# Hybrid encoder block on one core: the second group's queries and keys projected chunk by chunk, each chunk followed by its two head pairs

## The chip, the core and the metric

The kernel runs on one core of one Trainium2 chip. The metric is the device time of one execution in microseconds (us). The kernel before took 1394.3 us (median of three runs, 1393.5 to 1394.34).

## The reference, cut to what matters

The block takes `x` of 256 tokens by 2048 channels. One input projection gives the operands of a recurrent branch (HGRN2), the queries, keys and values of an attention branch, and two gates. The two branches are projected back, weighted by the gates, summed and projected once more; a squared-ReLU MLP follows. The change touches the attention branch only:

```python
s = jnp.einsum('bhnqd,bhnkd->bhnqk', qc, kb).astype(jnp.float32) * (Dh ** -0.5) + bias[:, None]
s = jnp.where(valid[:, None, :], s, -jnp.inf)
p = jax.nn.softmax(s, axis=-1).astype(v.dtype)
o = jnp.einsum('bhnqk,bhnkd->bhnqd', p, vb)
```

There are 16 heads of 64 channels. Head h has a bias of its own, gathered from a table by relative distance.

## The kernel before, in words

**Arithmetic.** Every large product is made in split precision. A weight piece of 128 x 1024 numbers comes from DRAM into a `raw` tile, ScalarE rounds it to a high part (`wh`, line 91), and VectorE subtracts to get the low part (`wl`, line 92). `wh` and `wl` have four buffers each, `raw` has six. TensorE then multiplies high by high, high by low and low by high.

**Stages around the change.** After the recurrent branch come the attention's projections. A query or key *chunk* is 256 channels, that is four heads or two *head pairs*: `qk_chunk` streams 16 K-tiles of weights through TensorE (lines 177 and 182), 64 matmuls in all, and then evicts the sum into a tile `aq..T` or `ak..T` by one ScalarE copy (line 189) and two VectorE operations (190, 304). The two *groups* of the code are channels 0 to 511 (heads 0 to 7) and 512 to 1023 (heads 8 to 15). In the trace of the kernel before, `aq10T` is the first query chunk of the second group, `ak11T` its second key chunk. The loop before is: for each group, both query chunks, both key chunks, (in the first group) the value projection `av`, then the group's four head pairs. After the second group come the gate projections, of which `ga0` is the first (products on lines 135 to 137, named `acc_ga0c`).

**One head pair.** `attn_pair` writes the scores of two heads into the PSUM tile `s` (line 588, eight matmuls; the tile has one buffer). For each head, `attn_head` then loads the bias by a DMA that GpSimd issues (594) into one of three buffers, masks a corner (memset, 595), adds the bias to the two parts of the scores (597, 598), takes two maxima (600, 601), exponentiates with a running sum on ScalarE (603, 604), takes reciprocals (606) and scales (607, 608), all but 603 and 604 on VectorE. TensorE transposes the result in three pieces into `tpp` (611) and ScalarE copies that to `pt` (613). `attn_values` multiplies by the values into `pa` (624, eight matmuls), one pair later in the loop, and the result is split into `act_yb` (91, 92).

**What sets the order.** Each engine works through its own list of instructions in order. A scheduler writes these lists when the kernel is built; it moves independent work together, so a head pair's small operations stand among the large products of the code that follows it. Weight loads are issued by SyncE (`raw_..`), the bias loads by GpSimd. GpSimd also issues the accumulating transfers of a gate unit (line 789: `raw_ga0B` += `raw_ga0C`, and `rawd_ga0D` += `raw_ga0A`), each of 512 KB. A gate unit further copies one accumulator from PSUM on the way (`u_ga`, line 752), and the next product into the same pair of accumulators follows behind that copy.

In the trace and below the heads of the second group are called head 8 to head 15, and its pairs are pair 4 (heads 8 and 9) to pair 7 (heads 14 and 15).

Of the kernel before, what the change touches and what calls it, by code (L numbers as in the profile page):

```python
# [17 lines left out]
T = 256  # L18
# [4 lines left out]
NC = 512  # L23
# [9 lines left out]
C_HQ, C_HF, C_AQ, C_AK, C_GA, C_GB = 0, HG, 2 * HG, 3 * HG, 4 * HG, 4 * HG + D  # L33
# [17 lines left out]
def tile_hybrid_block(  # L51
# [38 lines left out]
    def split(hi, lo, src, copy=None):  # L90
        casts[:] = [(copy or nc.scalar.copy)(hi, src)]  # L91
        return nc.vector.tensor_tensor(lo, src, hi.bitcast(F32), op=ALU.subtract)  # L92
# [7 lines left out]
    def new_act(what):  # L100

        return apool.tile([P, 4, 2, T], F32R, name=f"act_{what}", tag="act")
# [60 lines left out]
    def gemm_t(rhs, w, n0, nkt, what):  # L163

        acc = new_acc(what)
        for a in weights(w, n0, nkt, T, what):
            tick(1)
            mm_t(acc, rhs, nkt, *a)
        return acc
# [45 lines left out]
    for kt, n in zip(starts, steps):  # L215
# [3 lines left out]
        with tc.high_priority(offset=2000):  # L219
            for j in range(n):  # L220
                g, hi = wmix[:, kt + j:kt + j + 1], xT[c][:, a + j, 0, :]
# [10 lines left out]
    def rows(factors, what):  # L232

        wide = hp.tile([P, NM, P], F32, name=f"wide_{what}", tag="wide", bufs=1)
        nc.vector.tensor_copy(wide, bc(factors, 2, P))
        tp = ps_tp.tile([P, NM, P], F32, name=f"tp_{what}", tag="tp")
        for m in range(NM):
            nc.tensor.transpose(tp[:, m, :], wide[:, m, :], ident)
        r = const.tile([P, T], F32, name=f"rows_{what}")
        nc.vector.tensor_copy(r, tp.rearrange("p m t -> p (m t)"))  # L240
        return r
# [50 lines left out]
    rstd_t = rows(rstd, "rstd")  # L292
    rstd8_t = const.tile([P, T], F32, name="rstd8_t")
# [7 lines left out]
    def z_t(col, what, dst, factor, acc=None):  # L301

        add_parts(dst, acc or gemm_t(xT, w_in_t, col, KD, what))
        nc.vector.tensor_tensor(dst, dst, bc(factor, 1, 2), op=ALU.mult)
        return dst
# [256 lines left out]
    acc_q = [gemm_t(xT, w_in_t, C_AQ + i * T, KD, f"aq0{i}") for i in range(2)]  # L562
# [12 lines left out]
    yb = []  # L575
    TOK = 11

    def qk_chunk(col, what, factor, acc=None):
        return z_t(col, what, bp.tile([P, 2, T], F32, name=f"{what}T", tag="qk", bufs=6), factor, acc)

    def attn_pair(g, pr, qT, kT):

        sc = ps_sc.tile([P, 2, NC], F32, name=f"s{g}{pr}", tag="sc")
        with tc.high_priority(offset=2000):
            for d, q, k in ((slice(0, P), slice(0, P), slice(0, P)), (slice(P, 3 * P), slice(P, T), slice(0, T))):
                for j in range(2):
                    r = slice(64 * j, 64 * j + 64)
                    nc.tensor.matmul(sc[:, j, d], qT[r, q], kT[r, k], start=True, stop=True)
        return [attn_head(g * 8 + 2 * pr + j, sc[:, j, 0:3 * P]) for j in range(2)]
# [26 lines left out]
    def attn_values(g, pr, pts, vs):  # L616

        hi, lo = yb[g][:, :, 0, :], yb[g][:, :, 1, :]
        po = ps_tp.tile([P, T], F32, name=f"pa{g}{pr}", tag="tp")
        with tc.high_priority(offset=2000):  # L620
            for i, src, dst in ((0, slice(0, 2), slice(0, T)), (1, slice(2, 3), slice(P, T))):
                for j, pt in ((1, pts[1]), (0, pts[0])):
                    r = slice(64 * j, 64 * j + 64)
                    nc.tensor.matmul(po[r, dst], vs[i][:, P * pr + 64 * j:P * pr + 64 * j + 64], pt[:, src, :].rearrange("p a t -> p (a t)"),
                                     start=i == 0, stop=i == 1, skip_group_check=True)
        split(hi[:, pr, :], lo[:, pr, :], po)
# [300 lines left out]
    av = [[None] * NM for _ in range(2)]  # L927
# [5 lines left out]
    def alone(u, then=None):  # L933
        run(u, then)
        flush()
        pairs.clear()

    for g in range(2):
        qT = [qk_chunk(C_AQ + g * NC + i * T, f"aq{g}{i}", rstd8_t, None if g else acc_q[i]) for i in range(2)]
        kT = [qk_chunk(C_AK + g * NC + i * T, f"ak{g}{i}", rstd_t) for i in range(2)]  # L940
        if not g:
            alone(Unit(lambda: xT, lambda: Sx, w_in_n, C_AV, "av", values))
        yb.append(new_act(f"yb{g}"))
        pts = None
        for pr in range(5):
            last = pts
            if pr < 4:
                pts = attn_pair(g, pr, qT[pr // 2][:, pr % 2, :], kT[pr // 2][:, pr % 2, :])
            if last:
                attn_values(g, pr - 1, last, av[g])  # L950

    ga, gb = [], []
    units = []
# [124 lines left out]
    for qd in range(NQ):  # L1078
        last = qd == NQ - 1
# [121 lines left out]
```

## Time and profile before

| | us |
|---|---|
| median of three runs | 1394.3 |
| the profiled execution | 1393.71 |
| its span (first to last instruction) | 1392.0 |
| TensorE clock granted in it | 0.998 |
| chunks of the second group, first matmul of `aq10` to last of `ak11` | 307 to 361 |
| gate unit `ga0`, from its first matmul to that of `ga2` | 361 to 415 |

Busy time and idle time are in microseconds, start times count from the span's start. TensorE's matmuls overlap, so a row's duration is longer than the distance to the next row: a wait on TensorE is read from the distance between two starts. Where the trace names a releaser in square brackets, the engine was idle for the time given there.

### The profile page before, as it was taken

What the parts mean: (1) busy time and instruction counts of PE and PEld (TensorE: products, weight loads), DVE (VectorE), ACT (ScalarE), POOL (GpSimd) and SP (SyncE); (2) the same over time, 40 slices, a digit from 0 to 9 for tenths busy, and PEclk for the clock granted to TensorE, in tenths of its full rate; (3) what the DMA queues carried; (4) which work ended last, traced back from release to release, by engine and by line L of the source; (5) the groups of instructions that cost most, each with busy time, mean ns of one, the idle gap of its engine ahead of it and who ended that gap; (6) DMA issues with size and microseconds to landing.
All of it is one profiled execution on the core that took longest, in us unless ns stands there. A gap on an engine that the chain in (4) does not pass through costs nothing.

```text
span 1392.0 us, 18634 instructions
## 1 busy us (share of the span) xinstructions
PE 1377.6 (99%) x6550; PEld 1142.7 (82%) x6550; DVE 1138.1 (82%) x1429; ACT 925.9 (67%) x1193; POOL 144.8 (10%) x231
## 2 busy tenths in 40 slices
PE   9999999999999999999999999999999999999997
PEld 7889888878778888888888888888888888888886
DVE  7897997975978785687998977879877897878885
ACT  6774765664766664346777776678666876668864
POOL 2000001100100000001211001100011001110200
PEclk9999999999999999999999999999999999999999
DMA  9654445784758896558989789997899888999892
GB/s 332 231 174 157 155 165 180 220 282 161 185 183 270 263 268 229 193 169 269 277 233 314 243 258 291 268 268 237 249 295 293 251 241 246 275 294 269 255 285 100
DMA packets 124078, 331.62 MB, mean 238 GB/s; under 512 B 11072, under 2 KB 11840, under 8 KB 123600
## 3 DMA queue, kind: packets, MB, share of 16 engines
q1 hardware_dynamic: 103696, 265.59, 54.1%
q0 software_dynamic: 19568, 64.04, 23.4%
q8 instruction: 51, 0.84, 0.2%
q10 hardware_dynamic: 720, 0.81, 0.2%
q14 instruction: 43, 0.35, 0.1%
HBM read 271.67 MB, written 10.49 MB: 203 GB/s over the span
## 4 chain that ended last, share of the span: by engine, by line
PE 93%; DVE 2%; issue 2%; DMA 1%; ACT 1%; POOL 0%; SPq 0%; POOLq 0%; ACTq 0%; DVEq 0%
PE acc_hf L177 2%; PE acc_ak L177 2%; PE acc_aq L177 2%; PE acc_hq L177 2%; PE ps L414 1%; PE tp_u L108 1%; PE acc_hg L136 1%; PE acc_bb L136 1%; PE acc_hg L135 1%; PE acc_ba L136 1%; PE acc_bb L137 1%; PE acc_ba L137 1%; PE acc_hg L137 1%; PE acc_bb L135 1%; PE acc_ba L135 1%
## 5 line engine op out<-in xcount | busy, mean ns | idle before, releaser
L177 PE MATMUL acc_aq<-act_x,wh_aq 128*128 128x512 f32 x128 | 41.8, 406 | 0.0
L177 PE MATMUL acc_hf<-act_x,wh_hf 128*128 128x512 f32 x128 | 41.0, 402 | 0.2 <-DVE wh_hf L91 0.2
L177 PE MATMUL acc_hq<-act_x,wh_hq 128*128 128x512 f32 x128 | 40.7, 399 | 0.0
L177 PE MATMUL acc_ak<-act_x,wh_ak 128*128 128x512 f32 x128 | 40.5, 397 | 0.1
L91 ACT CAST wh_bb<-raw_bb 128x1024 fp32r<-128x1024 f32 x16 | 16.9, 1054 | 23.3 <-PE acc_ba L137 17.7
L92 DVE TENSOR_TENSOR wl_bb<-raw_bb,wh_bb 128x1024 fp32r<-128x1024 f32 x16 | 19.6, 1223 | 14.8 <-ACT wh_bb L91 14.8
L91 ACT CAST wh_ba<-raw_ba 128x1024 fp32r<-128x1024 f32 x16 | 16.8, 1053 | 21.0 <-PE acc_bb L137 13.8
L92 DVE TENSOR_TENSOR wl_ba<-raw_ba,wh_ba 128x1024 fp32r<-128x1024 f32 x16 | 19.6, 1224 | 12.7 <-ACT wh_ba L91 12.7
L91 ACT CAST wh_aq<-raw_aq 128x1024 fp32r<-128x1024 f32 x16 | 16.8, 1051 | 19.4 <-PE acc_hg L137 8.8
L182 PEld LDWEIGHTS acc_hq<-act_x,wl_hq 128*128 128x128 f32 x128 | 23.4, 188 | 6.5 <-DVE wl_hq L92 1.3
L182 PEld LDWEIGHTS acc_hf<-act_x,wl_hf 128*128 128x128 f32 x128 | 23.4, 188 | 6.1 <-DVE wl_hf L92 0.9
L182 PEld LDWEIGHTS acc_ak<-act_x,wl_ak 128*128 128x128 f32 x128 | 23.5, 188 | 5.5 <-issue 0.3
L182 PEld LDWEIGHTS acc_aq<-act_x,wl_aq 128*128 128x128 f32 x128 | 23.6, 189 | 5.0
L92 DVE TENSOR_TENSOR wl_aq<-raw_aq,wh_aq 128x1024 fp32r<-128x1024 f32 x16 | 19.6, 1223 | 9.2 <-ACT wh_aq L91 9.2
L92 DVE TENSOR_TENSOR wl_hf<-raw_hf,wh_hf 128x1024 fp32r<-128x1024 f32 (+2 forms) x21 | 20.4, 969 | 6.9 <-ACT wh_hf L91 6.8
L91 ACT CAST wh_hf<-raw_hf 128x1024 fp32r<-128x1024 f32 (+1 forms) x19 | 16.9, 890 | 13.5 <-PE acc_hg L137 6.0
L92 DVE TENSOR_TENSOR wl_ak<-raw_ak,wh_ak 128x1024 fp32r<-128x1024 f32 x16 | 19.6, 1222 | 7.7 <-ACT wh_ak L91 7.7
L135 PE MATMUL acc_hi<-wh_hi,act_x 128*128 128x512 f32 x64 | 25.8, 403 | 0.0
L92 DVE TENSOR_TENSOR act_u<-tp_u,act_u 128x512 fp32r<-128x512 f32 x32 | 22.0, 686 | 4.7 <-ACT act_u L91 4.2
L98 POOL TENSOR_TENSOR ro<-ms,mhalf 128x2 f32<-128x2 f32 x8 | 5.9, 738 | 190.2 <-DVE ms L97 190.2
L135 PE MATMUL acc_hg<-wh_hg,act_x 128*128 128x512 f32 x64 | 25.7, 401 | 0.0
L182 PE MATMUL acc_hq<-act_x,wl_hq 128*128 128x256 f32 x128 | 24.7, 279 | 0.9 <-DVE wl_hq L92 0.9
(1928 smaller groups left out, 5267.4 us busy)
## 6 DMA issues: line engine op xcount, KB each, us to landing
raw_hi<-in_w_in_n_dram SPq DMA_DIRECT2D x16, 512.0 KB, 4.0
raw_hg<-in_w_in_n_dram SPq DMA_DIRECT2D x16, 512.0 KB, 3.6
raw_aq<-in_w_in_t_dram SPq DMA_DIRECT2D x16, 512.0 KB, 4.1
raw_ak<-in_w_in_t_dram SPq DMA_DIRECT2D x16, 512.0 KB, 3.6
raw_ba<-in_w_branch_a_dram SPq DMA_DIRECT2D x16, 512.0 KB, 4.6
raw_bb<-in_w_branch_b_dram SPq DMA_DIRECT2D x16, 512.0 KB, 4.6
raw_hf<-in_w_in_t_dram SPq DMA_DIRECT2D x12, 512.0 KB, 3.6
raw_hq<-in_w_in_t_dram SPq DMA_DIRECT2D x12, 512.0 KB, 3.7
```

What stands on the lines that cost most here:

```text
L91: casts[:] = [(copy or nc.scalar.copy)(hi, src)]
L92: return nc.vector.tensor_tensor(lo, src, hi.bitcast(F32), op=ALU.subtract)
L98: nc.gpsimd.tensor_tensor(dst, ms, mhalf[:, :width], op=ALU.pow)
L108: nc.tensor.transpose(tp[:, j, :], src[:, j * P:(j + 1) * P], ident)
L135: nc.tensor.matmul(acc, hi, wh, start=first, stop=False, skip_group_check=True)
L136: nc.tensor.matmul(acc, hi, wl, start=False, stop=False, skip_group_check=True)
L137: nc.tensor.matmul(acc, lo, wh, start=False, stop=last, skip_group_check=True)
L177: nc.tensor.matmul(acc[:, cb, :], wh[:, cb * P:(cb + 1) * P], r.rearrange("p u t -> p (u t)"), start=kt == 0, stop=last)
L182: nc.tensor.matmul(acc[:, cb, 0:T], wl[:, cb * P:(cb + 1) * P], r[:, 0, :], start=False, stop=False)
L414: nc.tensor.matmul(ps[:, m, :], klf[:, a * P:(a + 1) * P], qrf[:, a * 192:(a + 1) * 192], start=True, stop=True)
```

## The change

The loop over groups becomes a loop over chunks. The first group's four chunks are projected first as before, with the value projection behind them. The first group's head pairs follow in the same order. In the second group the third query chunk and the third key chunk (channels 512 to 767) are projected and followed by pairs 4 and 5; then the fourth chunks (channels 768 to 1023), followed by pairs 6 and 7. The product with the values still comes one pair later, now also across the border between groups. The tiles are named `aq0T` to `aq3T` and `ak0T` to `ak3T`; before's `aq10T` is after's `aq2T`, `aq11T` is `aq3T`, `ak10T` is `ak2T` and `ak11T` is `ak3T`. No instruction is added or removed.

```diff
-    for g in range(2):
-        qT = [qk_chunk(C_AQ + g * NC + i * T, f"aq{g}{i}", rstd8_t, None if g else acc_q[i]) for i in range(2)]
-        kT = [qk_chunk(C_AK + g * NC + i * T, f"ak{g}{i}", rstd_t) for i in range(2)]
-        if not g:
+    qT = [qk_chunk(C_AQ + i * T, f"aq{i}", rstd8_t, acc_q[i]) for i in range(2)]
+    kT = [qk_chunk(C_AK + i * T, f"ak{i}", rstd_t) for i in range(2)]
+    pts = None
+    for i in range(4):
+        if i > 1:
+            qT.append(qk_chunk(C_AQ + i * T, f"aq{i}", rstd8_t))
+            kT.append(qk_chunk(C_AK + i * T, f"ak{i}", rstd_t))
+        if not i:
             alone(Unit(lambda: xT, lambda: Sx, w_in_n, C_AV, "av", values))
-        yb.append(new_act(f"yb{g}"))
-        pts = None
-        for pr in range(5):
-            last = pts
-            if pr < 4:
-                pts = attn_pair(g, pr, qT[pr // 2][:, pr % 2, :], kT[pr // 2][:, pr % 2, :])
+        if not i % 2:
+            yb.append(new_act(f"yb{i // 2}"))
+        for pr in (2 * i, 2 * i + 1):
+            last, pts = pts, attn_pair(pr // 4, pr % 4, qT[i][:, pr % 2, :], kT[i][:, pr % 2, :])
             if last:
-                attn_values(g, pr - 1, last, av[g])
+                attn_values((pr - 1) // 4, (pr - 1) % 4, last, av[(pr - 1) // 4])
+    attn_values(1, 3, pts, av[1])
```

How the instruction lists move is seen at three places.

**TensorE, the chunk in which pair 5's scores are made.** Before, this is the fourth key chunk (`acc_ak` with `ak10T` ready); `s_3655` are pair 5's scores, and nothing of the softmax follows them in the chunk:

```order
L177 MATMUL acc_ak_3513<-act_x_109,wh_ak_8_3559 128x512
L588 MATMUL s_3655<-ak10T,aq10T 128x128 x2
L588 MATMUL s_3655<-ak10T,aq10T 128x256 x2
L177 MATMUL acc_ak_3513<-act_x_109,wh_ak_8_3559 128x512
L182 MATMUL acc_ak_3513<-act_x_109,wl_ak_8_3560 128x256 x2
L177 MATMUL acc_ak_3513<-act_x_109,wh_ak_8_3559 128x512 x2
```

After, it is the fourth query chunk (`acc_aq`), and `s_3469` are pair 5's scores; `tpp_3434` and `tpp_3456` are the transposes of heads 8 and 9, `pa_3462` the first group's last product with the values:

```order
L177 MATMUL acc_aq_3526<-act_x_109,wh_aq_8_3572 128x512
L588 MATMUL s_3469<-ak2T,aq2T 128x128 x2
L588 MATMUL s_3469<-ak2T,aq2T 128x256 x2
L611 MATMUL tpp_3434<-ident,sb_3421 128x128 x3
L177 MATMUL acc_aq_3526<-act_x_109,wh_aq_8_3572 128x512
L182 MATMUL acc_aq_3526<-act_x_109,wl_aq_8_3573 128x256 x2
L177 MATMUL acc_aq_3526<-act_x_109,wh_aq_8_3572 128x512 x2
L611 MATMUL tpp_3456<-ident,sb_3443 128x128
L624 MATMUL pa_3462<-pt_3217,av_2968 64x256
```

The transposes of heads 8 to 11 all move from the gate unit `ga0` into the fourth query chunk; the fourth key chunk behind it is left without any attention work.

**TensorE, the end of the product `ga0p21B`, where `u_ga` is copied.** `ga0r_8` is the next product; before, its first matmul stands directly behind `ga0p21B`:

```order
L136 MATMUL acc_ga0c_3852<-wl_ga0p21B_4022,S_x 128x512
L137 MATMUL acc_ga0c_3852<-wh_ga0p21B_4021,S_x 128x512
L135 MATMUL acc_ga0c_3852<-wh_ga0r_8_4041,act_x_109 128x512
L611 MATMUL tpp_3788<-ident,sb_3775 128x128
L136 MATMUL acc_ga0c_3852<-wl_ga0r_8_4042,act_x_109 128x512
```

After, pair 7's product with the values (`pa_3823`) stands between the two:

```order
L136 MATMUL acc_ga0c_3852<-wl_ga0p21B_4022,S_x 128x512
L137 MATMUL acc_ga0c_3852<-wh_ga0p21B_4021,S_x 128x512
L624 MATMUL pa_3823<-pt_3814,av_3004 64x256
L624 MATMUL pa_3823<-pt_3792,av_3004 64x256
L624 MATMUL pa_3823<-pt_3814,av_3006 64x128
L624 MATMUL pa_3823<-pt_3792,av_3006 64x128
L135 MATMUL acc_ga0c_3852<-wh_ga0r_8_4041,act_x_109 128x512
```

So independent work has come between the product whose sum is copied and the product that goes on with it.

**GpSimd, around the accumulating transfers of `ga0`.** `bias_3738`, `bias_3772` and `bias_3794` are the biases of heads 13, 14 and 15:

```order
 L789 DMA raw_ga0B_3834<-raw_ga0C_3838 128x1024
-L595 MEMSET bias_3716 64x64
 L789 DMA raw_ga0B_3836<-raw_ga0C_3840 128x1024
 L789 DMA rawd_ga0D_3842<-raw_ga0A_3830 128x1024
+L594 DMA bias_3794<-in_rel_bias_dram 128x256
 L789 DMA rawd_ga0D_3844<-raw_ga0A_3832 128x1024
-L594 DMA bias_3738<-in_rel_bias_dram 128x256
-L595 MEMSET bias_3738 64x64
-L594 DMA bias_3772<-in_rel_bias_dram 128x256
-L595 MEMSET bias_3772 64x64
-L594 DMA bias_3794<-in_rel_bias_dram 128x256
 L595 MEMSET bias_3794 64x64
```

The loads for heads 13 and 14 have moved ahead of all four accumulating transfers, and the load for head 15 now stands behind one transfer of `rawd_ga0D` and ahead of the other.

## The prediction, made before the changed kernel ran

> **What bounds the kernel now.** First the page: busy shares, the granted clock, and the chain that ended last.
>
> ```profile
> PE 1377.6 (99%) x6550; PEld 1142.7 (82%) x6550; DVE 1138.1 (82%) x1429; ACT 925.9 (67%) x1193; POOL 144.8 (10%) x231
> ...
> PEclk9999999999999999999999999999999999999999
> ...
> PE 93%; DVE 2%; issue 2%; DMA 1%; ACT 1%; POOL 0%; SPq 0%; POOLq 0%; ACTq 0%; DVEq 0%
> ```
>
> TensorE carries the chain almost from end to end at an undisturbed clock. As the change leaves the number of instructions on every engine as it was, the only thing it can move is the time TensorE waits. So the second view is the windows of 10 us around the attention (columns: stretch, its length, then busy us and count for PE, PEld, DVE, ACT, POOL; clock, DMA share, GB/s).
>
> ```profile
> 310.00:320.00 10.00, 10.00 (x67) 7.18 (x63) 8.50 (x27) 7.36 (x23) 1.51 (x5) 1.00 0.47 144
> ...
> 340.00:350.00 10.00, 10.00 (x60) 8.76 (x58) 5.03 (x7) 4.13 (x5) 0.00 (x0) 1.00 0.60 206
> 350.00:360.00 10.00, 10.00 (x63) 7.91 (x63) 9.23 (x18) 4.65 (x10) 3.12 (x6) 1.00 0.49 119
> ...
> 370.00:380.00 10.00, 9.79 (x49) 7.39 (x48) 9.79 (x21) 8.09 (x15) 1.80 (x3) 1.00 1.00 234
> 380.00:390.00 10.00, 8.77 (x51) 6.23 (x53) 8.18 (x23) 7.21 (x20) 1.43 (x4) 1.00 0.90 306
> ```
>
> In the second group's plain chunks (340 to 350) VectorE is half idle. In `ga0` (from 361) it is nearly full, because the softmax of heads 10 to 15 lies there beside the gate weights' splits, and TensorE falls under 10. In 310 to 320 a chunk carries two pairs of the first group, and TensorE is still at 10.00. The third view, TensorE's rows in order of time, gives the waits their size (start, duration).
>
> ```profile
> 361.67 0.40 PE L136 MATMUL acc_ga0c<-wl_ga0p11A,act_x 128*128 128x512 f32 x1
> 362.15 0.33 PE L611 MATMUL tpp<-ident,sb 128*128 128x128 f32 x1
> ...
> 379.39 0.40 PE L136 MATMUL acc_ga0c<-wl_ga0p21A,S_x 128*128 128x512 f32 x1
> 380.02 0.30 PE L611 MATMUL tpp<-ident,sb 128*128 128x128 f32 x1 [0.23 <-DVE sb L607]
> ...
> 383.90 0.48 PE L135 MATMUL acc_ga0c<-wh_ga0r,act_x 128*128 128x512 f32 x1
> 384.31 0.93 PE L588 MATMUL s<-ak11T,aq11T 64*128 64x128 f32 x8
> ...
> 387.56 0.39 PE L137 MATMUL acc_ga0c<-wh_ga0p21B,S_x 128*128 128x512 f32 x1
> 389.16 0.33 PE L611 MATMUL tpp<-ident,sb 128*128 128x128 f32 x1 [1.21 <-DVE sb L607]
> 389.42 0.87 PE L624 MATMUL pa<-pt,av 128*64 128x256 f32 x8
> 390.22 0.44 PE L611 MATMUL tpp<-ident,sb 128*128 128x128 f32 x2
> ...
> 391.42 0.39 PE L136 MATMUL acc_ga0c<-wl_ga0p21B,S_x 128*128 128x512 f32 x1
> 391.65 0.40 PE L137 MATMUL acc_ga0c<-wh_ga0p21B,S_x 128*128 128x512 f32 x1
> 392.72 0.49 PE L135 MATMUL acc_ga0c<-wh_ga0r,act_x 128*128 128x512 f32 x1 [0.67 <-ACT u_ga L752]
> 393.22 0.30 PE L611 MATMUL tpp<-ident,sb 128*128 128x128 f32 x1
> ```
>
> Undisturbed, one matmul of 512 columns starts 0.23 us after the last (391.42 to 391.65). What exceeds that in front of a row is lost: 1.37 (387.56 to 389.16), 0.84 (391.65 to 392.72), 0.40 (379.39 to 380.02), 0.27 (392.72 to 393.22), 0.25 (361.67 to 362.15) and 0.18 (383.90 to 384.31), **3.31 us** together. Part of it is the ordinary price of a turn to another kind of matmul:
>
> ```profile
> 349.94 0.39 PE L177 MATMUL acc_ak<-act_x,wh_ak 128*128 128x512 f32 x1
> 350.26 0.93 PE L588 MATMUL s<-ak10T,aq10T 64*128 64x128 f32 x8
> ...
> 354.80 0.93 PE L588 MATMUL s<-ak10T,aq10T 64*128 64x128 f32 x8
> ```
>
> A turn to scores that wait for nothing costs 0.32 - 0.23 = 0.09. Five of the six places are turns (not 391.65), so 0.45 stays in any order, and **2.86 us is all that the change can win**.
>
> **Why TensorE waits there.** The largest wait is for head 13's scaling (607), which VectorE reaches only after head 14's bias has come. GpSimd's rows:
>
> ```profile
> 371.69 0.60 POOL L594 DMA_DIRECT2D bias<-in_rel_bias_dram  x1
> 380.04 0.19 POOL L595 MEMSET bias<- 64x64 f32 x1 [7.75 <-DMA bias<-in_rel_bias_dram]
> 380.58 0.56 POOL L594 DMA_DIRECT2D bias<-in_rel_bias_dram  x1 [0.35 <-POOL bias L595]
> 386.93 0.15 POOL L595 MEMSET bias<- 64x64 f32 x1 [5.79 <-DMA bias<-in_rel_bias_dram]
> ```
>
> Head 13's bias goes out at 371.69, right behind the accumulating transfers, and needs 8.35 us; head 14's stands behind its memset, goes out at 380.58 and needs 6.35. The Trainium skill, "DMA: Bandwidth & Descriptors", section "Anatomy of one DMA — SWDGE (gpsimd) path", fits such a load with about 2.0 us plus its bytes over 436 GB/s; for 128 KB that would be an estimated 2.3 us. By that rule no bias would be late in either kernel, and the last rival below would have no chance; the trace contradicts it with 8.35 and 6.35, so the rows decide.
>
> **The change, part by part.**
>
> *Loads, splits and projections in another order: nothing.* SyncE issues the same number of weight loads, and the third key chunk takes the place of the fourth query chunk with equal sizes. The cover is VectorE's idle half in plain chunks (5.03 of 10); without it, a late split of 1.22 us (row below) could stand in front of a matmul once per piece.
>
> *Head 14's late bias: -1.28 (1.37 less the turn).* Heads 13 and 14 now load ahead of all four accumulating transfers. Head 15's load stands behind one of them. Even at 8.35 us from about 9 us into `ga0` it is there at 17 to 18, some 4 us ahead of its place in VectorE's list, which I count at 21 to 22 from the rows before. So nothing of VectorE stands behind a bias here.
>
> *The copy `u_ga`: -0.74.* Pair 7's product with the values fills the pause. It takes 0.80 (389.42 to 390.22) of the 0.84; 0.1 I leave for its own `pt` copy coming just in time. Both ends: 0 to -0.84.
>
> *The other four turns to `tpp` and `s`: -0.74* (0.40 + 0.27 + 0.25 + 0.18 less 4 x 0.09): `ga0` carries four heads where it carried the softmax of six and the last transposes of two more.
>
> *New waits in the fourth query chunk: +0.35.* Here TensorE works under pair 4 and 5's softmax. Rows of the same sequence in the fourth key chunk of before:
>
> ```profile
> 352.73 1.23 DVE L92 TENSOR_TENSOR wl_ga0p11A<-raw_ga0A,wh_ga0p11A 128x1024 fp32r<-128x1024 f32 x1
> ...
> 351.65 1.05 ACT L91 CAST wh_ga0p11A<-raw_ga0A 128x1024 fp32r<-128x1024 f32 x1 [2.08 <-PE acc_ak L177]
> ...
> L607 DVE TENSOR_SCALAR sb<-sb,rs x16: 276/280/290, 270.4 to 398.8; 128x128 f32<-128x128 f32 x16
> ...
> 361.11 0.49 PE L611 MATMUL tpp<-ident,sb 128*128 128x128 f32 x3
> ```
>
> Count from pair 4's scores (350.26 there). The cast that follows a piece's last use comes at +1.4 (351.65), so that of the next piece, 4 x 0.70 later, at +4.2 or +4.3, and its split from +5.4 to +6.6. Head 9's reciprocal and scaling stand behind that split on VectorE; 0.2, a score addition of 0.2 and 0.28 later, at **+7.2**, TensorE may turn head 9. TensorE gets there at +4.54 (pair 5's scores), + 0.93, + about 0.5 (three transposes), + five matmuls, 0.93: **+6.9**. So it waits 0.35. The same count finds heads 10 and 11 ready 0.1 us before TensorE comes. Both ends: 0, as in the window 310 to 320, and 2.0, what the turns in `ga0` cost before (2.86 less 0.84). I stay near the first, since that window shows the same work under the same kind of chunk.
>
> *A new wait at head 12's transpose: +0.40.* In `ga0` the scores of pair 7 become possible when head 13's have been read; then VectorE splits two pieces of `ga0p21A` before it scales head 12:
>
> ```profile
> 372.54 2.36 DVE L92 TENSOR_TENSOR wl_ga0p21A<-raw_ga0A,wh_ga0p21A 128x1024 fp32r<-128x1024 f32 x2
> ```
>
> Head 12 is ready 2.36 + 0.28 = 2.6 after that point; TensorE comes after the scores (0.93 and a turn) and four matmuls, 2.0 to 2.3. That is 0.3 to 0.6; both ends 0 and 0.7.
>
> *The sum:* -1.28 - 0.74 - 0.74 + 0.35 + 0.40 = **-2.0**, and 0.1 back for smaller turns that now fall on VectorE's busiest places: **-1.9 us**. The profiled execution took 1393.71 (span 1392.0 and 1.7 around it), so it would take 1391.8. The median of the runs lies 0.6 above that execution, at 1394.3; against it I forecast **1392.4 us**.
>
> **The rivals.**
>
> *All waits go, none comes: -2.86, 1391.4.* For it speaks the window 310 to 320 with TensorE at 10.00; against it that VectorE's list in the fourth query chunk has a split in front of each head.
>
> *The waits only move: -0.1, 1394.2.* The five turns cost 2.0 for six heads in `ga0`, 0.33 each. If a head costs that wherever it stands, eight cost 2.7, and with the copy's pause filled the rest is -0.1. For it: the softmax is the same work, and a chunk with four splits and two pairs keeps VectorE at 8.50 of 10 in the window above. Against it: the largest of the turns came from the bias, not from VectorE's load.
>
> *Slower: head 11's bias comes late in the fourth query chunk.* It has to wait for head 8's buffer. In before:
>
> ```profile
> 352.46 0.54 POOL L594 DMA_DIRECT2D bias<-in_rel_bias_dram  x1 [28.50 <-DVE mx L601]
> 356.45 0.14 POOL L595 MEMSET bias<- 64x64 f32 x1 [1.02 <-DMA bias<-in_rel_bias_dram]
> ...
> DMA to landing us min/median/max: 3.4/4.3/8.3
> ```
>
> It goes out 2.2 after pair 4's scores and landed in 4.0, at +6.2; VectorE wants it at +8.4. Later than that, head 10's scaling stands behind it on VectorE, and the rest of the chunk behind head 10's transposes on TensorE. Each microsecond of landing over 6.1 is then one lost. From a landing of 8.0 it eats the gain of 1.9; at the slowest, 8.35, it costs 2.25 and the kernel ends 0.35 slower, at 1394.6; over 10.9 it would be more than 0.2% slower. For it: two of sixteen loads took over 6. Against it: both came behind accumulating transfers, and here none is ahead of it, with the DMA engines at 0.49 to 0.60.
>
> **How the numbers follow.** Chances: forecast 0.50, waits only move 0.20, all go 0.16, late bias 0.14. A measurement of this kernel can tell about 0.2%, 2.8 us, from no change. Faster than that needs all of 2.86: 0.16 and 0.02 from the forecast's edge, 0.18. Slower than that takes a landing over 10.9 or several late ones in the last rival: 0.08. The rest, 0.74, lies within. The range goes from 1391.0 (all waits gone, and 0.4 for the runs' own spread) to 1395.4 (a bias landing in 9.1, slower than any seen and 1.1 over the point where the gain is eaten), which leaves out some 2 in 10.
>
> **What would show it.** Head 13's and 14's bias loads issued before the accumulating transfers of `ga0` and landing within 5; no VectorE row waiting for a bias in `ga0`; the pause at `u_ga` filled by `pa`; TensorE at 9.5 or more in the window of the fourth query chunk, with one gap of some 0.35 at head 9, and a gap of 0.3 to 0.6 at head 12. A VectorE row in the fourth query chunk that waits for a bias would prove the last rival, gaps of 0.3 at each of the eight heads the second. A split that comes late in the fourth key chunk, or a change in TensorE's clock, would be outside all of them.

## The result, and the profile after

| | before | after |
|---|---|---|
| median of the runs, us | 1393.97 (14 runs, 1392.96 to 1398.71) | 1391.38 (14 runs, 1390.61 to 1392.81) |
| the profiled execution, us | 1393.71 | 1390.61 |
| its span, us | 1392.0 | 1388.9 |
| third query chunk's first matmul to `ga2`'s first, us | 107.50 | 105.20 |
| `ga2`'s first matmul to `gb0`'s first, us | 36.39 | 35.91 |

The ratio of the times is **0.9982**, 95% interval 0.9975 to 0.9989: 2.6 us less, 1.5 to 3.5. The forecast was 1392.4, which was 1.9 less than the 1394.3 that was on record for before. The last two rows of the table are differences of start times in the traces. The first of them, called **the attention's stretch** below, holds all the work that the change moves (576 matmuls in both kernels), and it became **2.30 us** shorter. The second one turns out to vary by itself (below).

The page of the profile after, with TensorE's row and the shares of the chain that ended last, looks as before:

```profile
PE 1377.7 (99%) x6550; PEld 1144.0 (82%) x6550; DVE 1139.5 (82%) x1429; ACT 925.6 (67%) x1193; POOL 144.4 (10%) x231
...
PE 96%; DVE 2%; ACT 1%; issue 0%; DMA 0%; POOL 0%; SPq 0%; POOLq 0%; DVEq 0%; ACTq 0%
```

The busy times are those of before within 1.4 us; the chain's share of TensorE rose from 93% to 96%. The windows of 10 us (columns as in the prediction) show where TensorE is still short of 10:

```profile
340.00:350.00 10.00, 9.84 (x65) 7.49 (x64) 8.47 (x26) 7.56 (x23) 2.44 (x6) 1.00 0.73 199
...
370.00:380.00 10.00, 9.68 (x46) 7.11 (x46) 9.85 (x18) 7.81 (x15) 2.40 (x4) 1.00 0.93 213
380.00:390.00 10.00, 9.95 (x53) 7.15 (x53) 8.88 (x22) 7.93 (x17) 0.00 (x0) 1.00 0.91 303
```

The window 380 to 390, which lost 1.23 before (8.77 of 10), now loses 0.05; the fourth query chunk (340 to 350), which lost nothing when it was a key chunk, loses 0.16 under the softmax of four heads. TensorE's rows at the places that the prediction named:

```profile
344.08 0.63 PE L177 MATMUL acc_aq<-act_x,wh_aq 128*128 128x512 f32 x2
344.87 0.33 PE L611 MATMUL tpp<-ident,sb 128*128 128x128 f32 x1 [0.16 <-DVE sb L607]
...
377.50 0.40 PE L136 MATMUL acc_ga0c<-wl_ga0r,act_x 128*128 128x512 f32 x1
377.86 0.33 PE L611 MATMUL tpp<-ident,sb 128*128 128x128 f32 x1
...
383.99 0.39 PE L135 MATMUL acc_ga0c<-wh_ga0p21A,S_x 128*128 128x512 f32 x1
384.43 0.30 PE L611 MATMUL tpp<-ident,sb 128*128 128x128 f32 x1
...
391.99 0.40 PE L137 MATMUL acc_ga0c<-wh_ga0p21B,S_x 128*128 128x512 f32 x1
392.31 0.87 PE L624 MATMUL pa<-pt,av 128*64 128x256 f32 x8
393.11 0.50 PE L135 MATMUL acc_ga0c<-wh_ga0r,act_x 128*128 128x512 f32 x1
```

Beyond the pitch (0.23, the distance between two matmuls that wait for nothing) there are lost 0.33 ahead of head 9's transpose (the second of the two matmuls in the first row starts at 344.32), 0.13 at head 12's (377.50 to 377.86) and 0.21 at head 14's (383.99 to 384.43). The pause at `u_ga` is filled: pair 7's `pa` runs from 392.31 to 393.11, and the next product starts at once. GpSimd's rows, for the biases:

```profile
340.03 0.54 POOL L594 DMA_DIRECT2D bias<-in_rel_bias_dram  x1 [16.57 <-DVE mx L601]
...
344.00 0.14 POOL L595 MEMSET bias<- 64x64 f32 x1 [0.99 <-DMA bias<-in_rel_bias_dram]
...
347.23 1.08 POOL L594 DMA_DIRECT2D bias<-in_rel_bias_dram  x2 [0.36 <-DVE sb L598]
350.74 0.14 POOL L595 MEMSET bias<- 64x64 f32 x1 [2.43 <-DMA bias<-in_rel_bias_dram]
351.25 0.14 POOL L595 MEMSET bias<- 64x64 f32 x1 [0.36 <-DMA bias<-in_rel_bias_dram]
359.29 0.88 POOL L789 DMA_DIRECT2D raw_ga0B<-raw_ga0C  x1 [7.89 <-DMA raw_ga0C<-in_w_in_t_dram]
```

Heads 13 and 14 (the two issues at 347.23) have their biases by 351.25, 8 us ahead of the first accumulating transfer at 359.29. Head 11's, on which the slower rival rested, goes out at 340.03 and is masked at 344.00, in 4.0 us.

One pause in `ga0` stands in no list of the prediction and does not move: at the copy `acc_ga0c` (line 752) two products start 0.80 apart before (367.60 to 368.40) and 0.82 after (370.04 to 370.86), 0.57 and 0.59 over the pitch.

### The profile page after: what moved, and what is told of

The parts are those of the page before. It is cut to its first block, busy times and chain, and to the rows that moved or that the text cites. A ratio compares the mean times of both kernels' runs of the same rounds, so it can differ in the third digit from the quotient of the medians.

```text
span 1388.9 us, 18633 instructions
## 1 busy us (share of the span) xinstructions
PE 1377.7 (99%) x6550; PEld 1144.0 (82%) x6550; DVE 1139.5 (82%) x1429; ACT 925.6 (67%) x1193; POOL 144.4 (10%) x231
## 4 chain that ended last, share of the span: by engine, by line
PE 96%; DVE 2%; ACT 1%; issue 0%; DMA 0%; POOL 0%; SPq 0%; POOLq 0%; DVEq 0%; ACTq 0%
PE acc_ak L177 2%; PE acc_hf L177 2%; PE acc_aq L177 2%; PE acc_hq L177 2%; PE ps L414 1%; PE acc_ak L182 1%; PE tp_u L108 1%; PE acc_hg L136 1%; PE acc_hg L135 1%; PE acc_bb L135 1%; PE acc_bb L136 1%; PE acc_ba L135 1%; PE acc_ba L137 1%; PE acc_hg L137 1%; PE acc_ba L136 1%; PE acc_bb L137 1%
## 5 line engine op out<-in xcount | busy, mean ns | idle before, releaser
L182 PE MATMUL acc_aq<-act_x,wl_aq 128*128 128x256 f32 x128 | 25.8, 285 | 0.0
L135 PE MATMUL acc_bb<-wh_bb,act_yb 128*128 128x512 f32 x64 | 25.2, 393 | 0.0
L136 PE MATMUL acc_hi<-wl_hi,act_x 128*128 128x512 f32 x64 | 25.1, 392 | 0.0
```

Of the source, the lines that this page charges most:

```text
L135: nc.tensor.matmul(acc, hi, wh, start=first, stop=False, skip_group_check=True)
L136: nc.tensor.matmul(acc, hi, wl, start=False, stop=False, skip_group_check=True)
L182: nc.tensor.matmul(acc[:, cb, 0:T], wl[:, cb * P:(cb + 1) * P], r[:, 0, :], start=False, stop=False)
```

## The experiments

"Stretch" is the attention's stretch of the first table, from the traces; times are medians, with the ratio to the kernel before and its interval.

| kernel | time, us | ratio | stretch, us |
|---|---|---|---|
| before | 1393.97 | 1 | 107.50 |
| after | 1391.38 | 0.9982 (0.9975 to 0.9989) | 105.20 |
| before_5bias | 1392.20 | 0.9986 (0.9977 to 0.9995) | 105.95 |
| after_nofill | 1394.19 | 1.0001 (0.9992 to 1.001) | 106.00 |
| chunk_order_only | 1392.84 | 0.9991 (0.9982 to 1.0) | 105.74 |
| after_2bias | 1392.09 | 0.9986 (0.9977 to 0.9995) | 105.26 |
| after_5bias | 1391.77 | 0.9986 (0.9977 to 0.9995) | 105.15 |
| after_noborder | 1391.84 | 0.9982 (0.9973 to 0.9991) | 105.64 |
| after_cast | 1391.51 | 0.9985 (0.9977 to 0.9994) | 105.18 |
| after_prio | 1391.73 | 0.9978 (0.9969 to 0.9987) | not alike |
| after_1bias | 1408.47 | 1.0098 (1.0084 to 1.0112) | not alike |
| before_nomax | 1418.0 | 1.0164 (1.015 to 1.0178) | not alike |
| after_again | 1391.82 (1 run) | | 105.14 |
| before_again | 1399.14 (1 run) | | 112.96 |

In the three rows "not alike" eight matmuls of a product with the values (0.80 us) had moved ahead of the stretch. The intervals reach some 1.2 us to each side, so for kernels less than that apart the stretch decides, and it comes from one execution each; in two executions of the changed kernel it was 0.06 apart.

### The late bias alone: before_5bias

```diff
-        return z_t(col, what, bp.tile([P, 2, T], F32, name=f"{what}T", tag="qk", bufs=6), factor, acc)
+        return z_t(col, what, bp.tile([P, 2, T], F32, name=f"{what}T", tag="qk", bufs=5), factor, acc)
-        bias = bp.tile([P, T], F32, name=f"bias{hd}", tag="bias", bufs=3)
+        bias = bp.tile([P, T], F32, name=f"bias{hd}", tag="bias", bufs=5)
```

> The kernel before with five bias buffers in place of three (and five of the 2 KB query/key buffers in place of six, for room). The order of the chunks and pairs stays. Theory (the late bias behind the accumulating transfers of ga0 costs TensorE 1.3 us): the biases of heads 13 and 14 go out before those transfers, no VectorE row waits for a bias at 387, the gap of 1.37 in front of a transpose is gone, about 1.3 us less than before, 1392.7; the pause of 0.84 at the copy u_ga stays. Rival (VectorE's load in ga0 makes the waits, the bias only happens to be named): the gap stays within 0.3, 1394.0.

Measured: 1392.2, and 1.55 less in the stretch. From 300 to 420 us the lists of TensorE, VectorE and ScalarE hold the same rows in the same order as before; what moves is GpSimd's loads. VectorE's row at head 14's bias in the kernel before, and then the same row and the issue of head 14's load here:

```profile
387.11 0.29 DVE L597 TENSOR_TENSOR sb<-s,bias 128x128 f32<-128x128 f32 x1 [1.52 <-POOL bias L595]
```

```profile
385.40 0.28 DVE L597 TENSOR_TENSOR sb<-s,bias 128x128 f32<-128x128 f32 x1
```

```profile
354.81 0.54 POOL L594 DMA_DIRECT2D bias<-in_rel_bias_dram  x1 [1.91 <-issue]
```

Head 13's load goes out at 352.36 and head 14's at 354.81, ahead of all four accumulating transfers (the first at 356.86), and VectorE's wait of 1.52 is gone. TensorE's rows at head 13's transposes and at the pause:

```profile
387.45 0.39 PE L137 MATMUL acc_ga0c<-wh_ga0p21B,S_x 128*128 128x512 f32 x1
387.68 0.27 PE L611 MATMUL tpp<-ident,sb 128*128 128x128 f32 x1
...
390.12 0.40 PE L137 MATMUL acc_ga0c<-wh_ga0p21B,S_x 128*128 128x512 f32 x1
391.19 0.50 PE L135 MATMUL acc_ga0c<-wh_ga0r,act_x 128*128 128x512 f32 x1 [0.67 <-ACT u_ga L752]
```

The 1.37 in front of head 13's transpose is gone (387.45 to 387.68 is the bare pitch), the pause at `u_ga` stays at 0.84, and so do three of the four other gaps (0.26, 0.41, 0.18). The fourth, 0.27 behind the pause, fell to 0.11, little over a turn: it was head 14's transpose, and before, ahead of that head's scaling, VectorE waited another 0.34 (391.12) for head 15's bias, the last of the same row of loads; the trace itself names no releaser for this gap. So the theory holds, and the late biases had cost 1.55, not 1.28. Two thirds of the change's gain come from the loads' place in GpSimd's list.

The two late loads were not slow for the same reason. The DMA view by queue shows it in the kernel before, from 372 to 378 and from 380.6 to 384.7 (q0 carries GpSimd's transfers, q1 SyncE's weight loads; packets, MB, share of the 16 engines' time):

```profile
q0 software_dynamic: 246, 0.88, 90.6%
```

```profile
q1 hardware_dynamic: 625, 1.21, 92.8%
```

Head 13's load (371.69) has the accumulating transfers ahead of it in its own queue, and q0 takes nine tenths of the DMA engines' time. Head 14's (380.58) can go out only when head 13's has landed and been masked; by then the accumulating transfers are over. In its first 4 us no packet of q0 moves at all, while weight loads fill the engines. So it was late because of the list, and slow beside weight loads; that these held it up is a reading of one view, and no run took them away.

### The filled pause alone: after_nofill

Pair 7's product with the values is put behind the products that follow the pause, near the end of `ga0`, so that it can't fill it:

```diff
-        with tc.high_priority(offset=2000):
+        with tc.issue_after(behind.ins) if behind else tc.high_priority(offset=2000):
...
-    attn_values(1, 3, pts, av[1])
...
+    attn_values(1, 3, pts, av[1], mark[0])
```

> The kernel after, with pair 7's product with the values held back until the product ga0r_8 is done, so that nothing stands between ga0p21B and ga0r_8. Theory (pa fills the pause at u_ga): the gap of about 0.84 in front of ga0r_8 is back, about 0.8 us more than after, 1392.2. Rival (the pause came from ScalarE being busy before and is gone anyway): no gap over 0.2, 1391.4.

```profile
392.72 0.40 PE L137 MATMUL acc_ga0c<-wh_ga0p21B,S_x 128*128 128x512 f32 x1
393.79 0.50 PE L135 MATMUL acc_ga0c<-wh_ga0r,act_x 128*128 128x512 f32 x1 [0.68 <-ACT u_ga L754]
...
416.76 0.39 PE L775 MATMUL acc_ga2c<-act_x 128*128 128x512 f32 x1
418.15 0.50 PE L135 MATMUL acc_ga2c<-wh_ga2p22A,S_x 128*128 128x512 f32 x1 [1.01 <-DVE act_yb L92]
```

The pause is back (392.72 to 393.79, 0.84 over the pitch) and the stretch is 0.80 longer: the term of 0.74 holds, a little small. The rest of the loss is another thing: the moved product is now split into `act_yb` when `ga2` has begun, ScalarE's and VectorE's lists are other ones there, and TensorE waits once for 1.0 (418.15). So the whole time, back at before's, overstates the pause: 0.80 of it belongs to the pause, 1.48 to the stretch behind, and the rest of the 2.8 between the medians was not traced.

### The order of the projections alone: chunk_order_only

```diff
+    qT = [qk_chunk(C_AQ + i * T, f"aq{i}", rstd8_t, acc_q[i]) for i in range(2)]
+    kT = [qk_chunk(C_AK + i * T, f"ak{i}", rstd_t) for i in range(2)]
     for g in range(2):
...
+        else:
+            for i in range(2, 4):
+                qT.append(qk_chunk(C_AQ + i * T, f"aq{i}", rstd8_t))
+                kT.append(qk_chunk(C_AK + i * T, f"ak{i}", rstd_t))
```

> The projections in the new order (third query and key chunk, then the fourth), but all four head pairs of the second group behind them as before. Theory (what counts is where the scheduler puts the softmax and the bias loads): heads 10 to 15 stay in ga0, heads 14 and 15 load behind the accumulating transfers, waits of 2 to 3 us remain there, 1393.4 to 1394. Rival (the order of the projections alone makes the gain): 1391.4.

Measured: 1392.84, and 1.76 less in the stretch: more than the theory gave to the mere order. All four pairs still stand behind both chunks in the code, but pair 4's operands are there earlier: its scores are made at 339.65 instead of 350.26, and the transposes of both its heads stand at the end of the fourth key chunk (361.67), where before had those of head 8 alone (361.11). Apart from the pause at the copy `acc_ga0c`, no gap over 0.45 is left but the one at `u_ga` (0.91): head 13's load has moved ahead of the last two accumulating transfers (364.18, the first of these two at 370.17). VectorE still waits 0.90 for head 15's bias (388.26), at a place where TensorE has other work. So the number that was expected fell, and the rows tell the parts apart: here the order of the projections suffices against the late bias of heads 13 and 14, and `pa` did not come into the pause, as it does in the changed kernel, where the pairs also follow their chunks.

### How much room the loads have: after_5bias, after_2bias, after_1bias

```diff
-        bias = bp.tile([P, T], F32, name=f"bias{hd}", tag="bias", bufs=3)
+        bias = bp.tile([P, T], F32, name=f"bias{hd}", tag="bias", bufs=2)
```

and the same with 1, and with 5 (there `qk` has five buffers instead of six).

> The changed kernel with five bias buffers instead of three (and five query and key tiles instead of six): the lists of TensorE, VectorE and ScalarE are the same row for row, only GpSimd's loads go out earlier, all of them ahead of ga0's accumulating transfers. Theory, that no bias was late any more in the changed kernel: the same within 0.2, 1391.4, with head 9's 0.33, head 12's 0.14 and head 14's 0.22 all still there. Rival, that part of these still comes from a bias: head 14's 0.22 and head 12's 0.14 go, 1391.0.

> The kernel after with two bias buffers in place of three, so each load waits for the head two back and goes out later; heads 14 and 15 load behind accumulating transfers again. Theory (a bias that comes late on VectorE's list is passed on to TensorE in full): VectorE rows waiting for a bias in the fourth query chunk or in ga0, a gap of 0.5 to 2 us behind them, 1392 to 1393.4. Rival (the bias has slack everywhere and the gain came from VectorE's lighter load in ga0): no such row, 1391.4.

> The kernel after with one bias buffer, so every head's load goes out only when the head ahead of it has been added; heads 13, 14 and 15 load behind accumulating transfers of ga0 again, one after the other. Theory (a bias that lands late holds VectorE's list, and TensorE's transposes behind it): VectorE rows in ga0 or in the fourth query chunk wait for a bias, and TensorE shows gaps of 1.5 us or more together behind them; 1393 to 1397. Rival (bias loads have slack everywhere): no such gaps, 1391.4 to 1391.9.

With five buffers the stretch is the same (105.15 for 105.20) and head 9's 0.33, head 12's 0.13 and head 14's 0.22 are all there: no bias was late any more in the changed kernel. With two the stretch is also the same (105.26), and the expected wait of 0.5 to 2 in the fourth query chunk or in `ga0` did not come. Head 14's load goes out at 373.12 there instead of 347.23, between the two transfers of `rawd_ga0D`, and head 15's at 376.50, behind all four; they take 4.9 and 7.1 us and are still in time. Only in the first group does VectorE wait for two biases (0.48 and 0.26), with a gap of 0.38 on TensorE behind them. So a load behind an accumulating transfer costs nothing as long as VectorE comes later than its landing. With one buffer the loads can't run ahead at all. The waits of VectorE, and then those of TensorE (columns: total us, times, longest us), between 300 and 420 and between 300 and 450:

```profile
DVE sb L597 <- POOL bias L595: 12.7, 7, 2.1
```

```profile
PE tpp L611 <- DVE sb L607: 8.3, 6, 2.6
```

VectorE waits for seven biases, and TensorE behind it for six heads, 8.3 us in all. This is the slower rival's mechanism, and it is real; the changed kernel is far from it (head 11's load took 4.0, and 6.1 was the limit). The 1393 to 1397 expected was too little: the first group's heads lose as well; the stretch begins 8.65 later than in the changed kernel, of which the product that moved ahead of it explains 0.80. Two pauses of TensorE here, 3.24 (284.8 to 288.1) and 2.57 (325.0 to 327.6), also halved its clock for a while; the last section has the rows.

### Is it VectorE's work? before_nomax

```diff
-        mx = small.tile([P, 2], F32, name=f"mx{hd}", tag="mx")
-        nc.vector.tensor_reduce(mx[:, 0:1], s[:, 0:P], axis=AX.X, op=ALU.max, negate=True)
-        nc.vector.tensor_reduce(mx[:, 1:2], s[:, P:], axis=AX.X, op=ALU.max, negate=True)
+        mx = mhalf[:, 0:2]
...
-        nc.scalar.activation(s[:, 0:P], s[:, 0:P], AF.Exp, bias=mx[:, 0:1], accum_out=sums[:, 0:1])
+        nc.scalar.activation(s[:, 0:P], s[:, 0:P], AF.Exp, bias=mx[:, 0:1], scale=0.001, accum_out=sums[:, 0:1])
...
```

> The kernel before without the two maxima per head (the softmax leaves out the maximum and shrinks its exponent), which takes some 0.5 us per head from VectorE and leaves heads 14 and 15 loading behind the accumulating transfers. Theory: the gaps at turns shrink with VectorE's load (0.40, 0.25 and 0.18 to 0.1 or less over an ordinary turn), but a gap behind a late bias, 0.8 us or more, stays in ga0, and the pause of 0.84 at u_ga. Rival (VectorE's load alone): every gap but that pause goes.

TensorE's and VectorE's rows at the late bias in that kernel:

```profile
386.52 0.40 PE L135 MATMUL acc_ga0c<-wh_ga0p21A,S_x 128*128 128x512 f32 x1
389.30 0.30 PE L609 MATMUL tpp<-ident,sb 128*128 128x128 f32 x1 [2.38 <-DVE sb L605]
```

```profile
387.80 0.29 DVE L597 TENSOR_TENSOR sb<-s,bias 128x128 f32<-128x128 f32 x1 [2.75 <-POOL bias L595]
```

Without the two maxima (0.28 and 0.41 by their rows before, about 0.5 from start to start) the wait is longer, not shorter: VectorE itself stands idle for 2.75 at a bias, and TensorE's gap is 2.55 over the pitch. The bias is head 15's here, whose load goes out at 383.70, behind the mask of head 14's (383.16). The pause at `u_ga` stays at 0.84. So the large wait was not VectorE being full. The smaller ones can't be read off this kernel, since its order is another one: the 0.25 and the 0.18 are gone from their places, another 0.18 stands ahead of a product with the values, and 0.53 stands where 0.40 stood. Its time says nothing here: TensorE's matmuls of 512 columns follow each other at a median of 231 ns in it instead of 227, through the whole kernel, at the same granted clock of 0.998. Why was not found.

### Head 9's 0.33: after_noborder, after_prio, after_cast

Three attempts on the largest of the gaps that are left. The first takes away the product with the values that crosses the border between the groups, the second puts the scaling (606 to 608) ahead in the lists, the third puts ScalarE's cast of the fourth key chunk's second piece behind head 9's exponentials:

```diff
+        if i == 1:
+            attn_values(0, 3, pts, av[0])
+            pts = None
```

```diff
+        with tc.high_priority(offset=4000):
+            nc.vector.reciprocal(rs, sums)
...
```

```diff
-                with tc.high_priority(offset=2000):
+                with tc.issue_after(exps[9].ins) if (what, k0) == ("ak3", 4) else tc.high_priority(offset=2000):
                     split(wh[:, a:a + n], wl[:, a:a + n], raw[:, a:a + n], nc.vector.tensor_copy if n == 1 and not beside else None)
```

> The kernel after, but the first group's last product with the values stays in front of the third query chunk, as before the change. Theory (crossing the group's border moves one product and nothing that waits): within 0.3 us of after, 1391.4, with the gap of 0.33 at head 9 in place. Rival (that product in the fourth query chunk is part of the gain or of what is left of the loss): the gap at head 9 or 10 changes by over 0.2.

> The kernel after, with each head's reciprocal and scaling (lines 606 to 608) ahead of the weights' splits in the scheduler's priorities. Theory (what is left are heads whose scaling stands behind a split on VectorE): the gaps at heads 9, 12 and 14 (0.33, 0.14 and 0.22) go under 0.1 over a turn, about 0.4 us less than after, 1391.0. Rival (the splits are then late in their turn): gaps in front of the weights' matmuls, 1391.4 or more.

> The changed kernel, but ScalarE's cast of the fourth key chunk's second weight piece (wh_ak_4) is put behind head 9's exponentials instead of ahead of them; VectorE's split of it then comes behind the scalings of heads 9 and 10. Theory that head 9's 0.33 us is a chain through that cast and split (the exponential stands behind the cast, 1.05, and the scaling behind the split, 1.22): the gap before head 9's first transpose goes, 0.3 less, 1391.1. Rival, that it is the price of head 9's softmax wherever it stands, because VectorE's own work takes as long: the gap stays at 0.3 or moves to head 10, 1391.4. A late split of wh_ak_4 would show as a gap at the fourth key chunk's second piece; the cover there is some 15 us.

None of them removed it. Without the crossing product head 9's gap stays at 0.33, and 0.26 is added at head 11; the stretch is 0.44 longer, more than the 0.3 that was allowed for. With the early scaling it stays at 0.33, head 12's is gone, but the scheduler's order also changed at `u_ga`: pair 7's `pa` now stands two matmuls ahead of the end of `ga0p21B`, and the pause of 0.84 is back. The time is the same within the interval, so the expected 0.4 was not gained. In after_cast the gap is even 0.42. TensorE's and VectorE's rows there:

```profile
344.28 0.48 PE L177 MATMUL acc_aq<-act_x,wh_aq 128*128 128x512 f32 x1
344.93 0.33 PE L611 MATMUL tpp<-ident,sb 128*128 128x128 f32 x1 [0.17 <-DVE sb L607]
```

```profile
344.38 0.17 DVE L606 RECIPROCAL rs<-sum 128x2 f32<-128x2 f32 x1 [0.73 <-ACT sb L604]
344.58 0.29 DVE L607 TENSOR_SCALAR sb<-sb,rs 128x128 f32<-128x128 f32 x1
```

Counted from pair 5's scores (343.12 here, 342.37 in the changed kernel), head 9's scaling starts at +1.46 instead of +2.17. So the theory's chain through the cast and the split is right: without it head 9 is ready 0.7 us earlier. But the transposes moved too: they now stand behind one matmul of the chunk instead of five, and TensorE gets to them 0.8 earlier. It comes too early by 0.1 more than before, which is the difference between 0.33 and 0.42. The gap is not set by how soon the head is ready alone, but by where the scheduler puts the transposes against it, and the theory left that out.

### Each kernel once more: after_again, before_again

> The changed kernel once more, for one question: whether the pause at u_ga of ga2 (0.30 in the profiled execution of the kernel before, none in that of the changed one) varies between executions of one kernel. If it does: some other value than 0 here, up to 0.6. If it belongs to the kernel: 0 again.

> The kernel before once more, for the same question: if the pause at u_ga of ga2 varies between executions of one kernel, another value than 0.30; if it belongs to the kernel, 0.30 again. The gaps of ga0 (1.37, 0.84, 0.40, 0.27, 0.25, 0.18) should all be there within 0.1.

The changed kernel repeats: stretch 105.14, gaps 0.33, 0.15 and 0.22, no pause in `ga2`. The kernel before, by an execution of 1399.14, shows what its late bias can cost. GpSimd's and TensorE's rows, and the clock by windows:

```profile
372.13 0.59 POOL L594 DMA_DIRECT2D bias<-in_rel_bias_dram  x1
381.33 0.14 POOL L595 MEMSET bias<- 64x64 f32 x1 [8.60 <-DMA bias<-in_rel_bias_dram]
381.87 0.56 POOL L594 DMA_DIRECT2D bias<-in_rel_bias_dram  x1 [0.39 <-POOL bias L595]
388.88 0.14 POOL L595 MEMSET bias<- 64x64 f32 x1 [6.46 <-DMA bias<-in_rel_bias_dram]
```

```profile
388.00 0.39 PE L137 MATMUL acc_ga0c<-wh_ga0p21B,S_x 128*128 128x512 f32 x1
391.11 0.48 PE L611 MATMUL tpp<-ident,sb 128*128 128x128 f32 x1 [2.72 <-DVE sb L607]
...
393.91 0.63 PE L136 MATMUL acc_ga0c<-wl_ga0p21B,S_x 128*128 128x512 f32 x1
394.34 0.63 PE L137 MATMUL acc_ga0c<-wh_ga0p21B,S_x 128*128 128x512 f32 x1
```

```profile
388.00:392.00 4.00, 1.28 (x6) 0.48 (x5) 2.82 (x9) 2.03 (x6) 0.68 (x2) 0.85 0.75 263
392.00:396.00 4.00, 4.00 (x16) 2.62 (x12) 2.69 (x6) 1.59 (x3) 0.14 (x1) 0.50 0.41 132
396.00:401.00 5.00, 4.33 (x12) 3.21 (x12) 3.02 (x6) 2.38 (x5) 0.00 (x0) 0.50 0.46 148
401.00:405.00 4.00, 4.00 (x18) 3.05 (x17) 1.62 (x4) 1.57 (x4) 0.00 (x0) 1.00 0.21 77
```

Head 13's bias took 9.20 instead of 8.35, head 14's, which waits behind it, 7.01 instead of 6.35: 1.51 in sum. The gap on TensorE grew by just that, from 1.37 to 2.88. After the idle 2.72 TensorE then ran at a granted clock of 0.50 until 401, its matmuls 0.43 apart instead of 0.23, and `ga0` as a whole took 5.45 longer than in the other execution of the same kernel. The expectation "within 0.1" was missed here, and the miss is the finding: two loads in a row that together took 1.5 us more made `ga0` 5.5 longer. The gaps ahead of it (0.25, 0.40, 0.18) are the same to 0.01.

As for `ga2`: the second execution of before has no pause there and takes 35.92 from `ga2`'s to `gb0`'s first matmul, as the changed kernel does. The pause comes from a weight load. ScalarE's rows of the kernel before:

```profile
435.40 1.05 ACT L91 CAST wh_ga2r<-rawp_ga2r 128x1024 fp32r<-128x1024 f32 x1 [2.83 <-DMA rawp_ga2r<-in_w_in_t_dram]
436.35 2.00 ACT L91 CAST wh_ga2p21D<-rawd_ga2D 128x1024 fp32r<-128x1024 f32 x2
438.26 0.57 ACT L752 COPY u_ga<-acc_ga2c 128x512 f32<-128x512 f32 x1
```

The copy `u_ga` stands behind three casts, and the first of them waited 2.83 for its load. The 0.48 by which this stretch was shorter in the profile after is therefore no part of the change.

## Why the prediction was right

The forecast was 1.9 us less within a range of 1391.0 to 1395.4; the runs gave 2.6 less (1.5 to 3.5) and the traces 2.30 in the stretch that the change touches. The mechanism was right, and two sizes in the sum were off by more than 0.2. Point by point:

- **What bounds the kernel**: TensorE's waits, found by the distance of its rows. It held: the busy times of every engine stayed, and the gain is the sum of gaps that went, less those that came.
- **What can be won, 2.86**: it left out the pause of 0.57 at the copy `acc_ga0c`, which the change did not touch. It also took 0.09, the price of a turn to scores, for every turn; turns to a transpose that is ready came out between 0.00 (387.45 to 387.68 in before_5bias) and 0.09.
- **Head 14's late bias, -1.28**: right in cause, shown by before_5bias, and too small: 1.55. The prediction counted the wait at head 13's transpose and put head 14's transpose behind it (0.27) among the other turns, while it fell to 0.11 with the loads alone. That both loads were slow behind accumulating transfers was right for head 13's only; beside head 14's the queues show weight loads.
- **The copy `u_ga`, -0.74**: right; in after_nofill 0.80 comes back.
- **The other turns, -0.74**: too large. The 0.27 of them went with the biases; the other three were 0.83 together, less 3 x 0.09 leaves 0.56. That they went can be read in the rows; that VectorE's lighter load in `ga0` did it was not tested by itself.
- **Head 9's new wait, +0.35**: 0.33 was measured at the very place, of which 0.09 is an ordinary turn. The chain was the one that was counted, cast, split, then scaling: the split runs at +5.3 to +6.5 (+5.4 to +6.6 was expected), and the scaling is done at 344.82, 6.98 after the scores at 337.84, where +7.2 was expected. TensorE also came 0.2 earlier than counted, at +6.7, so the difference held.
- **Head 12's new wait, +0.40**: the mis-sized term. It measured 0.13, little over a turn. The sum had TensorE begin pair 7's scores when they become possible; by the rows it was busy then and came to them half a microsecond later, while VectorE's two splits took what was counted.
- **Left out**: head 14's 0.21 (its scaling stands behind a split of `ga0p21B` and the split of `act_yb` and ends at 384.29; the trace names no releaser), about 0.1 over a turn, which is what was put back for smaller turns.
- **The sum by these sizes**: -1.55 - 0.80 - 0.56 + 0.24 + 0.04 + 0.12 = -2.51; the stretch measured -2.30, the 0.2 between was not traced to single places. The forecast had taken the gain too small at the bias (0.27), at head 12 (0.36) and at head 9 (0.11), and too large at the turns (0.18).

Of the rivals, **all waits go** (1391.4) has the time that came, but not its mechanism: waits of 0.33, 0.13 and 0.21 did come, and what brought the median there was the bias's greater cost and, as far as can be told, the runs' spread. **Waits only move** falls: the changed kernel's gaps are 0.68 for eight heads, not 0.33 each. **The late bias of head 11** did not happen, since its load landed in 4.0; after_1bias shows that the mechanism exists.

What stays open: 2.6 in the medians against 2.30 in the traces is inside the interval, so no cause can be given. One possible part is that the kernel before pays more than 1.55 for its late bias in some executions: of its 88 executions in the comparisons 12 took over 1395.0, of the changed kernel's 14 none (1392.81 at most). None of the twelve was profiled; the one profile of before in such an execution is before_again (1399.14). So this is argued, not shown.

## What to carry to other kernels

When a small engine issues loads in a list of its own, look where in that list each load stands, and behind which waits and transfers: here a 128 KB load behind two 512 KB transfers, and a second one that could go out only when the first had landed, made TensorE, at 99% busy, wait for 1.5 us, and two more buffers or another order of the work removed it alike. What decides is not the place alone but whether the load lands before it is wanted: in after_2bias loads behind the same transfers cost nothing. Look also for what can stand between a product and the copy of its result: a pause of 0.84 was filled by 0.80 of work that had to be done anyway. A gap in front of an instruction depends on two times, that at which its data is ready and that at which the engine's list comes to it; making the data earlier by 0.7 won nothing here, since the list came to it 0.8 earlier.

## What the runs showed of the hardware beyond the expected

- **A pause of about 2.6 us on TensorE can halve its clock for longer than the pause.** Idle 2.72 (before_again) it was granted 0.50 for some 10 us; idle 2.57 (after_1bias) it fell as well, in the second row below; idle 2.38 (before_nomax) it did not: the matmuls at 390.37 and 390.60 there are again 0.23 apart. In after_1bias a pause of 3.24 that ended at 288.06 did it too: by windows of 4 us from 284 on the clock was 0.91, 0.50 and 0.73, which makes 6.9 us at half. Worked out the same way, the rows below give 3.4 us and those of before_again 10.2.

```profile
324.00:328.00 4.00, 1.43 (x10) 0.99 (x8) 1.89 (x7) 1.29 (x3) 0.14 (x1) 1.00 0.59 164
328.00:332.00 4.00, 4.00 (x16) 3.27 (x14) 2.37 (x7) 1.36 (x5) 0.54 (x1) 0.57 0.38 92
```

  The Trainium skill, "TensorE: Matmul & The Clock Gate", section "Part 1: The HAM clock gate", has the clock halve after an idle window of about 3.4 us that runs freely. Halving and the way back agree with the traces, and the three stretches at half clock are about one, two and three times 3.4; the idle time that suffices was shorter here, 2.57.
- **The same load takes another time in another execution.** Head 13's bias took 8.35 and 9.20 in two executions of the kernel before, with the same transfers ahead of it; all 16 loads together have a median of 4.3 and 4.1.
- **GpSimd's queue can stand still while weight loads fill the DMA engines.** Head 14's load of the kernel before was issued at 380.58, and from 380.6 to 384.7 none of its packets moved, with SyncE's queue at 92.8% of the engines' time; it landed after 6.35. In before_again it was the same from 381.9 to 385.8, with 88.2%. In the changed kernel two loads issued at 347.23 had both landed by 351.25.
- **A weight load's landing decides a pause elsewhere**: 0.30 at `ga2`'s `u_ga` in one execution of before, none in the other; the other kernels had between 0 and 0.61 there.
